# Two transformer blocks on one core: the opening rewritten, and the epsilon of the norms added on VectorE

## The chip, the cores and the metric

The kernel runs on one core of a Trainium2 chip. Its time is the device time of one execution in microseconds, and of several executions the median. Its engines work beside one another and meet at semaphores: TensorE (PE, matrix products and transposes, with weight loads as PEld), VectorE (DVE), ScalarE (ACT), GpSimd (POOL) and SyncE (SP), which here issues DMA transfers.

## The reference, cut to what matters

The input x is 256 tokens by 1024 channels, all in fp32. Two blocks run one after the other; each normalises, mixes and feeds forward with residuals. The first begins like this:

```
def rms_norm(x, gain):
    y = xf * lax.rsqrt(jnp.mean(xf * xf, axis=-1, keepdims=True) + RMS_EPS)
    return y * gain
h = rms_norm(x, g_mix_pre)
q, k, v, p, gu, gv, gates = split(h @ w_in)     # w_in is 1024 x 5376
```

Then come a stick-breaking attention in blocks of 128 tokens, a pooling over several windows, a gated spatial mixing, and a feed-forward part with norms before and behind it (`g_ff_pre`, `g_ff_post`). The second block is a transformer block whose norms are shifted and scaled by rows that come from a condition vector through a 1024-wide matrix (ada).

## The kernel before, in words

The 256 tokens are two tiles of 128 (t = 0, 1), kept token by partition as x0 and x1. A norm goes over one tile: ACT squares two halves of 512 channels with a running sum (`norm_stats`, line 530), POOL adds the two sums and epsilon (line 515) and raises the result to -1/2 (line 518), and DVE multiplies (lines 537 and 542 for a plain norm, 537 and 544 for a shifted one, 551 and 555 for a norm behind a branch). PE then transposes the tile in eight pieces of 128x128 (line 493), since its products want channels on partitions. Each transposed half is split into a high and a low part: hH by ACT (line 487), hL by DVE (line 488).

Weights stream from memory into three slots of 1 MB (`raw`, line 331), in a fixed list. `prep_one` makes of each a high part (ACT, line 352) and a low part (DVE, line 353), in two halves of 128x1024; four slots hold these. A product of fp32 numbers is made of three: high by high, low by high, high by low (lines 441 to 443, and 448 to 450 for the form with tokens on the output's partitions). The ada matrices are no products; DVE accumulates them (line 367).

The framework's scheduler puts the instructions of an engine in order, from the program's own order and costs of its own; slots and semaphores do the rest. Inside `tc.manual_schedule(engines=...)` the engines that are named keep the program's order. All loads go through SP in the order in which they are issued, and a slot's next load is issued when the conversion that reads it is done.

The opening: SP loads x0, then the row `g_mix_pre` spread over 128 partitions (512 KB, line 269), the first quarter of the weights for v, x1 behind it (line 333), and the rest. Then the two tiles are normalised (`make_h`) and the v products run: 48 of 128x512 from two weight slots, whose results are in two banks of PSUM. POOL makes the masks of the pooling part (lines 588 to 596) when the scheduler finds room. Behind v come products for p, gv, u, q, k, then the attention.

Of the kernel before, what the change touches and what calls it, by code (L numbers as in the profile page):

```python
# [105 lines left out]
def net_kernel(ctx: ExitStack, tc: tile.TileContext, I, out):  # L106
# [14 lines left out]
    def T(shape, tag, bufs, dt=F32):  # L121
        if tag in BASE_PAD and tag not in based:
            based.add(tag)
            sb.tile([P, BASE_PAD[tag]], F32, tag="pad" + tag, bufs=1, name=nm("pad"))
        return sb.tile(shape, dt, tag=tag, bufs=bufs, name=nm(tag))
# [7 lines left out]
    def dram(ap, offset, dims):  # L133
        return bass.AP(tensor=ap.tensor, offset=ap.offset + offset, ap=dims)
# [61 lines left out]
    B = {}  # L196
    B["v"] = block512(w_in, 5376, 1024)
    for h in range(2):
        stream[h].parts = [(0, 2), (2, 4)]
        stream[h].loads = [(dram(w_in, (h * 512 + a * P) * 5376 + 1024, [[5376, P], [P * 5376, 2], [1, 512]]), a, a + 2)  # L200
                           for a in (0, 2)]
    ada_want(0, (1, 0, 2, 4, 3, 5))
# [60 lines left out]

    x = [T([P, D], f"x{t}", 1) for t in range(NT)]
    xv = I["x"]
    nc.sync.dma_start(x[0], dram(xv, 0, [[D, P], [1, D]]))

    def bcast_row(tile_ap, vec, off, n, eng=None):
        (eng or nc.sync).dma_start(tile_ap, dram(vec, off, [[0, P], [1, n]]))
# [1 line left out]
    def gain_tile(vec):  # L271
        g = T([P, D], "gb", 2)
        bcast_row(g, vec, 0, D)
        return g

    ident = T([P, P], "ident", 1)
    make_identity(nc, ident)
    g_cur = gain_tile(I["g_mix_pre"])

    neg_half = T([P, 1], "neghalf", 1)  # L280
    nc.vector.memset(neg_half, -0.5)
# [42 lines left out]
    def issue_raw():  # L324
        while st["raw"] < len(stream) and st["raw"] < st["prep"] + RAW_SLOTS:
            it = stream[st["raw"]]
            rt = T([P, 2048], "raw", RAW_SLOTS)
            kc, n = it.shape if isinstance(it, Half) else (4, 512)
            v = rt.rearrange("p (c n) -> p c n", c=kc)
            for ap, a, b in it.loads:  # L330
                nc.sync.dma_start(v[:, a:b, :], ap)
                if st["raw"] == 0 and a == 0:
                    nc.sync.dma_start(x[1], dram(xv, P * D, [[D, P], [1, D]]))
            raws[st["raw"]] = v
            st["raw"] += 1

# [1 line left out]
    ada_tiles = {}  # L338
    ada_ready = []

    def prep_one():
        i = st["prep"]
        it = stream[i]
        v = raws.pop(i)
        if isinstance(it, Half):
            kc, n = it.shape
            h = T([P, kc, n], "wH", W_SLOTS, F32R)
            l = T([P, kc, n], "wL", W_SLOTS, F32R)
            for a, b in it.parts:
                m = (a + b) // 2  # L350
                for p, q in ((a, m), (m, b)) if b - a == kc else ((a, b),):
                    act(h[:, p:q, :], v[:, p:q, :], AF.Copy)  # L352
                    nc.vector.tensor_sub(l[:, p:q, :], v[:, p:q, :], h[:, p:q, :].bitcast(F32))  # L353
            it.H, it.L = h, l
            st["live"].append(it)
        else:
            if it.half == 0:
                ini = ada_init
                nc.sync.dma_start(ini[0:1, :], dram(I["ada_b_2"], it.layer * 6 * D + it.seg * D + it.n * 512,
                                                      [[512, 1], [1, 512]]))  # L360
                acc_cur[0] = T([P, 512], "acc", 1)
                src = ini
            else:
                src = acc_cur[0]
            for c in range(4):
                k = it.half * 4 + c
                stt(acc_cur[0], v[:, c, :], cond[:, k:k + 1], src, op0=ALU.mult, op1=ALU.add)  # L367
                src = acc_cur[0]
            if it.half == 1:
                ah = T([P, 512], "accH", 1, F32R)  # L370
                al = T([P, 512], "accL", 1, F32R)
                act(ah, acc_cur[0], AF.Copy)
                nc.vector.tensor_sub(al, acc_cur[0], ah.bitcast(F32))
                ada_ready.append((it, ah, al, st["gen"]))
        st["prep"] += 1
# [50 lines left out]
    def need(*blocks):  # L426
        pump()
        if any(h.H is None for b in blocks for h in b.halves):
            ada_finish()
            pump()  # L430
        for b in blocks:
            for h in b.halves:
                assert h.H is not None
# [78 lines left out]
    def rstd_of(parts):  # L512
        rs = T([P, 1], "rst", 4)
        if len(parts) == 2:
            nc.gpsimd.tensor_scalar(rs, parts[0], parts[1], EPS, op0=ALU.add, op1=ALU.add)  # L515
        else:
            nc.gpsimd.tensor_scalar(rs, parts[0], EPS, None, op0=ALU.add)
        nc.gpsimd.tensor_tensor(rs, rs, neg_half, op=ALU.pow)
        return rs

# [43 lines left out]

    hk = KM()
    issue_raw()
    for t in range(NT):
        make_h(hk, t, g_cur)
    pump()
    load_cols()  # L570
    load_cond()

    need(B["v"])
    vtok = T([P, NT, 512], "q4", 4)
    va = [bankA(), bankA()]
    for kq in range(4):
        for t in range(NT):
            ts(va[t], hk.h(t), hk.l(t), B["v"], K8[2 * kq:2 * kq + 2], 0, 512, start=(kq == 0), stop=(kq == 3))
    done(B["v"])
    for t in range(NT):  # L580
        act(vtok[:, t, :], va[t], AF.Copy)
# [27 lines left out]
    for g in range(4):  # L609
# [10 lines left out]
    nc.gpsimd.affine_select(tri, tri, pattern=[[-1, P]], base=0, channel_multiplier=1,  # L620
                            compare_op=ALU.is_ge, fill=0.0)


    wsT = T([P, 4, P], "ada5", 1)
    pt = bankB()
# [690 lines left out]
```

## Time and profile before

| | us |
|---|---|
| three runs | 1003.84, 1004.29 (median), 1008.91 |
| profiled execution | 1004.09 |
| its span, from first to last instruction | 1002.4 |
| PE busy in it | 966.3 |
| first transpose on PE | 11.00 |
| first v product | 16.12 |
| first p product | 28.20 |

The span is that of the trace; the execution is 1.69 us longer, with what starts and ends it. The mean granted clock of PE is 0.998 of full speed. The first p product marks the end of the opening: all v products have been issued by then. PE's busy time is not the whole of its span: the difference is idle time before and between instructions, which the waits list by what ended it. Times of places are given from the start of the span.

### The profile page before, as it was taken

The page shows a single profiled execution, that of the slowest core. Times are in us where ns is not written, and L with a number is a line of the kernel's source. Part 1 is how long each engine was busy: PE and PEld are TensorE (multiplying, and loading weights), DVE is VectorE, ACT ScalarE, POOL GpSimd, SP SyncE. Part 2 cuts the span into 40 slices and gives each one's busy share as a digit, 9 for nine tenths or more (in the row PEclk, how much of TensorE's full clock was granted, in tenths as well). Part 3 has the DMA queues.
Part 4 walks back from the last instruction along what each step waited for, and adds up shares of the span by engine and source line. Part 5 has one row for each costly group of instructions (what it writes and reads, how often), then busy time and mean ns, then how long its engine had stood idle before and what let it go on. Part 6 is the DMA issues. An engine that isn't in the chain of part 4 may idle for free.

```text
span 1002.4 us, 14398 instructions
## 1 busy us (share of the span) xinstructions
PE 966.3 (96%) x5733; PEld 837.2 (84%) x5733; DVE 716.6 (71%) x932; ACT 530.4 (53%) x777; POOL 66.6 (7%) x104
## 2 busy tenths in 40 slices
PE   4999999989999999999999999999999999999998
PEld 4999999868899997775778999997876778999996
DVE  6769887788577776889788567768678486665443
ACT  5656664357455455533556455545477456545451
POOL 5102010010000000100000000000330000000000
PEclk9999999999999999999999999999999999999999
DMA  8787686568777885677269777876534246577531
GB/s 270 249 295 251 221 295 207 183 222 307 249 243 283 284 300 204 210 262 274 84 211 305 274 260 252 284 252 210 169 125 169 84 145 233 210 242 252 198 128 43
DMA packets 102192, 223.99 MB, mean 223 GB/s; under 512 B 4332, under 2 KB 8326, under 8 KB 102125
## 3 DMA queue, kind: packets, MB, share of 16 engines
q1 hardware_dynamic: 102124, 223.07, 64.4%
q8 instruction: 45, 0.74, 0.3%
q14 instruction: 23, 0.18, 0.0%
HBM read 221.96 MB, written 1.10 MB: 223 GB/s over the span
## 4 chain that ended last, share of the span: by engine, by line
PE 82%; DVE 8%; POOL 3%; ACT 3%; issue 2%; DMA 1%; POOLq 0%; ACTq 0%; SPq 0%; DVEq 0%
PE A L443 14%; PE A L441 14%; PE A L442 14%; PE B L450 7%; PE B L449 7%; PE B L448 7%; PE A L448 4%; PE A L449 4%; PE A L450 3%; DVE wL L353 3%; ACT wH L352 1%; POOL rst L515 1%; ACT junk L530 1%; PE A L1028 1%; PE B L493 1%
## 5 line engine op out<-in xcount | busy, mean ns | idle before, releaser
L353 DVE TENSOR_TENSOR wL<-raw,wH 128x1024 fp32r<-128x1024 f32 x306 | 362.0, 1221 | 123.4 <-ACT wH L352 122.8
L352 ACT ACTIVATE wH<-raw 128x1024 fp32r<-128x1024 f32 x306 | 308.0, 1049 | 193.8 <-PE A L443 112.2
L450 PE MATMUL B<-hH,wL 128*128 128x256 f32 x576 | 163.0, 283 | 0.0
L449 PE MATMUL B<-hL,wH 128*128 128x256 f32 x576 | 163.0, 283 | 0.0
L448 PE MATMUL B<-hH,wH 128*128 128x256 f32 x576 | 162.9, 283 | 0.0
L441 PE MATMUL A<-wH,hidH 128*128 128x512 f32 x384 | 151.0, 393 | 0.0
L442 PE MATMUL A<-wL,hidH 128*128 128x512 f32 x384 | 150.2, 391 | 0.0
L443 PE MATMUL A<-wH,hidL 128*128 128x512 f32 x384 | 150.1, 391 | 0.0
L367 DVE SCALAR_TENSOR_TENSOR acc<-raw,cond,acc 128x512 f32<-128x512 f32 x168 | 125.9, 750 | 16.4 <-DMA raw<-in_ada_w_dram 13.0
L441 PE MATMUL A<-wH,hH 128*128 128x512 f32 (+1 forms) x336 | 130.5, 388 | 0.5 <-ACT hH L487 0.5
L443 PE MATMUL A<-wH,hL 128*128 128x512 f32 (+1 forms) x336 | 128.8, 383 | 0.2 <-DVE hL L488 0.2
L442 PE MATMUL A<-wL,hH 128*128 128x512 f32 (+1 forms) x336 | 128.8, 383 | 0.0
L449 PEld LDWEIGHTS B<-hL,wH 128*128 128x128 f32 x576 | 110.5, 192 | 0.7
L448 PEld LDWEIGHTS B<-hH,wH 128*128 128x128 f32 x576 | 110.5, 192 | 0.7
L450 PEld LDWEIGHTS B<-hH,wL 128*128 128x128 f32 x576 | 110.5, 192 | 0.0
L441 PEld LDWEIGHTS A<-wH,hidH 128*128 128x128 f32 x384 | 72.5, 189 | 15.4 <-issue 0.8
L443 PEld LDWEIGHTS A<-wH,hidL 128*128 128x128 f32 x384 | 72.5, 189 | 15.3
L442 PEld LDWEIGHTS A<-wL,hidH 128*128 128x128 f32 x384 | 72.6, 189 | 14.6
L448 PE MATMUL A<-hH,wH 128*128 128x256 f32 x272 | 77.8, 286 | 0.0
L449 PE MATMUL A<-hL,wH 128*128 128x256 f32 x272 | 77.0, 283 | 0.0
L450 PE MATMUL A<-hH,wL 128*128 128x256 f32 x272 | 76.9, 283 | 0.0
L441 PEld LDWEIGHTS A<-wH,hH 128*128 128x128 f32 x336 | 63.6, 189 | 13.7 <-issue 1.3
(234 smaller groups left out, 1287.9 us busy)
## 6 DMA issues: line engine op xcount, KB each, us to landing
raw<-in_mlp_w_dram SPq DMA_DIRECT2D x64, 1024.0 KB
raw<-in_ada_w_dram SPq DMA_DIRECT2D x48, 1024.0 KB
raw<-in_w_in_dram SPq DMA_DIRECT2D x19, 1024.0 KB
raw<-in_w_ff_in_dram SPq DMA_DIRECT2D x16, 1024.0 KB
raw<-in_w_ff_out_dram SPq DMA_DIRECT2D x16, 1024.0 KB
raw<-in_attn_w_qkv_dram SPq DMA_DIRECT2D x12, 1024.0 KB
raw<-in_conv_w_in_dram SPq DMA_DIRECT2D x8, 1024.0 KB
ada<-mod SPq DMA_DIRECT2D x24, 256.0 KB
```

What stands on the lines that cost most here:

```text
L352: act(h[:, p:q, :], v[:, p:q, :], AF.Copy)
L353: nc.vector.tensor_sub(l[:, p:q, :], v[:, p:q, :], h[:, p:q, :].bitcast(F32))
L367: stt(acc_cur[0], v[:, c, :], cond[:, k:k + 1], src, op0=ALU.mult, op1=ALU.add)
L441: mm(dst, lh(xc), wh, start=s0, stop=False)
L442: mm(dst, lh(xc), wl, start=False, stop=False)
L443: mm(dst, ll(xc), wh, start=False, stop=s1)
L448: mm(dst, wh, rh(xc), start=(i == 0), stop=False)
L449: mm(dst, wh, rl(xc), start=False, stop=False)
L450: mm(dst, wl, rh(xc), start=False, stop=(i == len(kcs) - 1))
L493: nc.tensor.transpose(pt[:, i * P:(i + 1) * P], src[:, i * P:(i + 1) * P], ident)
L515: nc.gpsimd.tensor_scalar(rs, parts[0], parts[1], EPS, op0=ALU.add, op1=ALU.add)
L530: act(junk(512), p, AF.Square, scale=1.0 / 32.0, accum_out=ss[:, n:n + 1])
```

## The change

It has two parts. The opening is rewritten. The gain row comes as one row of 4 KB, ahead of x0 and x1, which are loaded ahead of all weights. Two matmuls with a row of ones spread it over the 128 partitions into two banks of PSUM (`gp2`), and one DVE instruction per half multiplies x by the reciprocal root and by the gain. PE, DVE and ACT run in the order that is written there, POOL too up to the end of its masks. The first weights are converted in parts, and v products of tile 0 stand between. The other part is in `rstd_of`: the addition of epsilon is on DVE for all its callers, the power stays on POOL.

```diff
--- before.py
+++ after.py
@@ -196,7 +196,6 @@
     B = {}
     B["v"] = block512(w_in, 5376, 1024)
     for h in range(2):
-        stream[h].parts = [(0, 2), (2, 4)]
         stream[h].loads = [(dram(w_in, (h * 512 + a * P) * 5376 + 1024, [[5376, P], [P * 5376, 2], [1, 512]]), a, a + 2)
                            for a in (0, 2)]
     ada_want(0, (1, 0, 2, 4, 3, 5))
@@ -263,7 +262,10 @@
 
     x = [T([P, D], f"x{t}", 1) for t in range(NT)]
     xv = I["x"]
-    nc.sync.dma_start(x[0], dram(xv, 0, [[D, P], [1, D]]))
+    grow = T([1, D], "ada0", 1)
+    nc.sync.dma_start(grow, dram(I["g_mix_pre"], 0, [[D, 1], [1, D]]))
+    for t in range(NT):
+        nc.sync.dma_start(x[t], dram(xv, t * P * D, [[D, P], [1, D]]))
 
     def bcast_row(tile_ap, vec, off, n, eng=None):
         (eng or nc.sync).dma_start(tile_ap, dram(vec, off, [[0, P], [1, n]]))
@@ -275,7 +277,6 @@
 
     ident = T([P, P], "ident", 1)
     make_identity(nc, ident)
-    g_cur = gain_tile(I["g_mix_pre"])
 
     neg_half = T([P, 1], "neghalf", 1)
     nc.vector.memset(neg_half, -0.5)
@@ -329,8 +330,6 @@
             v = rt.rearrange("p (c n) -> p c n", c=kc)
             for ap, a, b in it.loads:
                 nc.sync.dma_start(v[:, a:b, :], ap)
-                if st["raw"] == 0 and a == 0:
-                    nc.sync.dma_start(x[1], dram(xv, P * D, [[D, P], [1, D]]))
             raws[st["raw"]] = v
             st["raw"] += 1
 
@@ -338,7 +337,7 @@
     ada_tiles = {}
     ada_ready = []
 
-    def prep_one():
+    def prep_one(by_part=False):
         i = st["prep"]
         it = stream[i]
         v = raws.pop(i)
@@ -346,13 +345,19 @@
             kc, n = it.shape
             h = T([P, kc, n], "wH", W_SLOTS, F32R)
             l = T([P, kc, n], "wL", W_SLOTS, F32R)
-            for a, b in it.parts:
-                m = (a + b) // 2
-                for p, q in ((a, m), (m, b)) if b - a == kc else ((a, b),):
-                    act(h[:, p:q, :], v[:, p:q, :], AF.Copy)
-                    nc.vector.tensor_sub(l[:, p:q, :], v[:, p:q, :], h[:, p:q, :].bitcast(F32))
             it.H, it.L = h, l
             st["live"].append(it)
+
+            def part(p, q):
+                act(h[:, p:q, :], v[:, p:q, :], AF.Copy)
+                nc.vector.tensor_sub(l[:, p:q, :], v[:, p:q, :], h[:, p:q, :].bitcast(F32))
+
+            m = kc // 2
+            if by_part:
+                st["prep"] += 1
+                return [lambda: part(0, m), lambda: part(m, kc)]
+            for p, q in ((0, m), (m, kc)):
+                part(p, q)
         else:
             if it.half == 0:
                 ini = ada_init
@@ -512,9 +517,9 @@
     def rstd_of(parts):
         rs = T([P, 1], "rst", 4)
         if len(parts) == 2:
-            nc.gpsimd.tensor_scalar(rs, parts[0], parts[1], EPS, op0=ALU.add, op1=ALU.add)
+            vts(rs, parts[0], parts[1], EPS, op0=ALU.add, op1=ALU.add)
         else:
-            nc.gpsimd.tensor_scalar(rs, parts[0], EPS, None, op0=ALU.add)
+            vts(rs, parts[0], EPS, None, op0=ALU.add)
         nc.gpsimd.tensor_tensor(rs, rs, neg_half, op=ALU.pow)
         return rs
 
@@ -564,18 +569,50 @@
 
     hk = KM()
     issue_raw()
-    for t in range(NT):
-        make_h(hk, t, g_cur)
+    vtok = T([P, NT, 512], "q4", 4)
+    va = [bankA(), bankA()]
+    pool_order = tc.manual_schedule(engines={nc.gpsimd.engine})
+    pool_order.__enter__()
+    with tc.manual_schedule(engines={nc.tensor.engine, nc.vector.engine, nc.scalar.engine}):
+        gp2 = [bankB(), bankB()]
+        for n in range(2):
+            mm(gp2[n], ones_r[0:1, :].bitcast(F32), grow[:, half(n)], start=True, stop=True)
+
+        def x_scaled(t, rs):
+            hs = []
+            for n in range(2):
+                h = T([P, 512], "rs", 4)
+                stt(h, x[t][:, half(n)], rs, gp2[n], op0=ALU.mult, op1=ALU.mult)
+                hs.append(h)
+            return hs
+
+        def v_part(t, kq):
+            ts(va[t], hk.h(t), hk.l(t), B["v"], K8[2 * kq:2 * kq + 2], 0, 512, start=(kq == 0), stop=(kq == 3))
+
+        rst = [norm_stats([x[0][:, half(n)] for n in range(2)])]
+        h0 = x_scaled(0, rst[0])
+        rst.append(norm_stats([x[1][:, half(n)] for n in range(2)]))
+        hk.from_token_half(0, 0, h0[0])
+        parts = prep_one(by_part=True)
+        parts[0]()
+        hk.from_token_half(0, 1, h0[1])
+        v_part(0, 0)
+        h1 = x_scaled(1, rst[1])
+        parts[1]()
+        issue_raw()
+        hk.from_token_half(1, 0, h1[0])
+        hk.from_token_half(1, 1, h1[1])
+        v_part(0, 1)
+        v_part(1, 0)
+        v_part(1, 1)
+        parts = prep_one(by_part=True)
+        for i in range(2):
+            parts[i]()
+            for t in range(NT):
+                v_part(t, 2 + i)
     pump()
     load_cols()
     load_cond()
-
-    need(B["v"])
-    vtok = T([P, NT, 512], "q4", 4)
-    va = [bankA(), bankA()]
-    for kq in range(4):
-        for t in range(NT):
-            ts(va[t], hk.h(t), hk.l(t), B["v"], K8[2 * kq:2 * kq + 2], 0, 512, start=(kq == 0), stop=(kq == 3))
     done(B["v"])
     for t in range(NT):
         act(vtok[:, t, :], va[t], AF.Copy)
@@ -620,6 +657,8 @@
     nc.gpsimd.affine_select(tri, tri, pattern=[[-1, P]], base=0, channel_multiplier=1,
                             compare_op=ALU.is_ge, fill=0.0)
 
+
+    pool_order.__exit__(None, None, None)
 
     wsT = T([P, 4, P], "ada5", 1)
     pt = bankB()
```

In the order of DVE in the opening, x_1_63 and x_2_64 are x0 and x1, gb_71 is the spread gain row, wL_149 and wL_132 the low part of the first weights. Before:

```order
L537 TENSOR_TENSOR rs_92<-x_1_63,gb_71 128x512
L537 TENSOR_TENSOR rs_94<-x_1_63,gb_71 128x512
L353 TENSOR_TENSOR wL_149<-raw_83,wH_148 128x1024
L542 TENSOR_SCALAR rs_92<-rs_92,rst_101 128x512
L542 TENSOR_SCALAR rs_94<-rs_94,rst_101 128x512
L537 TENSOR_TENSOR rs_120<-x_2_64,gb_71 128x512
L537 TENSOR_TENSOR rs_122<-x_2_64,gb_71 128x512
L542 TENSOR_SCALAR rs_120<-rs_120,rst_129 128x512
L542 TENSOR_SCALAR rs_122<-rs_122,rst_129 128x512
L488 TENSOR_TENSOR hL_82<-B_106,hH_81 128x4x128
L353 TENSOR_TENSOR wL_149<-raw_83,wH_148 128x1024
```

After, where B_100 and B_101 are the gain in PSUM and rst the norm's statistic:

```order
L520 TENSOR_SCALAR rst_109<-ss_104 128x1
L585 SCALAR_TENSOR_TENSOR rs_112<-x_1_63,rst_109,B_100 128x512
L585 SCALAR_TENSOR_TENSOR rs_114<-x_1_63,rst_109,B_101 128x512
L520 TENSOR_SCALAR rst_121<-ss_116 128x1
L493 TENSOR_TENSOR hL_83<-B_124,hH_82 128x4x128
L353 TENSOR_TENSOR wL_132<-raw_84,wH_131 128x1024
L493 TENSOR_TENSOR hL_83<-B_135,hH_82 128x4x128
L585 SCALAR_TENSOR_TENSOR rs_148<-x_2_64,rst_121,B_100 128x512
L585 SCALAR_TENSOR_TENSOR rs_150<-x_2_64,rst_121,B_101 128x512
L353 TENSOR_TENSOR wL_132<-raw_84,wH_131 128x1024
L493 TENSOR_TENSOR hL_83<-B_156,hH_82 128x4x128
```

The gain product and the scaling are one instruction, the additions of epsilon are DVE's, and the first half's weight subtraction stands behind hL of the first half of tile 0.

In the order of PE at the norm at 511 us of the trace before, A_4785 and A_4812 (after: A_4791 and A_4818) are banks of the second block's products, rs_4733 (after: rs_4739) the tile that waits to be transposed. Before:

```order
L443 MATMUL A_4785<-wH_4683,hL_4640 128x512
L441 MATMUL A_4785<-wH_4683,hH_4639 128x512
L442 MATMUL A_4785<-wL_4684,hH_4639 128x512
L493 MATMUL B_4747<-ident_66,rs_4733 128x128 x4
L443 MATMUL A_4785<-wH_4683,hL_4640 128x512
L493 MATMUL B_4754<-ident_66,rs_4735 128x128 x4
L441 MATMUL A_4812<-wH_4761,hH_4639 128x512
```

After:

```order
L448 MATMUL A_4791<-wH_4689,hL_4646 128x512
L446 MATMUL A_4818<-wH_4767,hH_4645 128x512
L447 MATMUL A_4818<-wL_4768,hH_4645 128x512
L448 MATMUL A_4818<-wH_4767,hL_4646 128x512
L446 MATMUL A_4818<-wH_4767,hH_4645 128x512
L447 MATMUL A_4818<-wL_4768,hH_4645 128x512
L498 MATMUL B_4753<-ident_69,rs_4739 128x128 x4
L448 MATMUL A_4818<-wH_4767,hL_4646 128x512
L498 MATMUL B_4760<-ident_69,rs_4741 128x128 x4
L446 MATMUL A_4818<-wH_4767,hH_4645 128x512
L447 MATMUL A_4818<-wL_4768,hH_4645 128x512
```

Products of the next bank, five of them, and one of the last have moved ahead of the first four transposes.

In the order of ACT at the norm at 204 us of the trace before, junk_2143 and junk_2145 are the squares of x0 (after: 2149 and 2151), hH_2122 (after: hH_2128) is the tile's high part, wH the weights' high parts. Before:

```order
L530 ACTIVATE junk_2143,ss_2142<-x_1_63 128x512
L352 ACTIVATE wH_2166<-raw_1905 128x1024
L530 ACTIVATE junk_2145,ss_2142<-x_1_63 128x512
L352 ACTIVATE wH_2174<-raw_2035 128x1024 x2
L487 ACTIVATE hH_2122<-B_2152 128x4x128
L487 ACTIVATE hH_2122<-B_2159 128x4x128
```

After:

```order
L352 ACTIVATE wH_2172<-raw_1911 128x1024 x2
L535 ACTIVATE junk_2149,ss_2148<-x_1_63 128x512
L535 ACTIVATE junk_2151,ss_2148<-x_1_63 128x512
L352 ACTIVATE wH_2180<-raw_2041 128x1024 x2
L352 ACTIVATE wH_2263<-raw_2178 128x1024 x2
L492 ACTIVATE hH_2128<-B_2158 128x4x128
L492 ACTIVATE hH_2128<-B_2165 128x4x128
```

Two weight copies, wH_2263 from raw_2178, now stand ahead of the two copies of hH.

## Rows read from the trace of the kernel before

**Rows 1.** Page, part 1: busy time by engine, share of the span, instructions.
```profile
PE 966.3 (96%) x5733; PEld 837.2 (84%) x5733; DVE 716.6 (71%) x932; ACT 530.4 (53%) x777; POOL 66.6 (7%) x104
```

**Rows 2.** Waits of PE by line: us in total, times, longest.
```profile
PE B L493 <- DVE rs L542: 16.7, 4, 11.0
PE B L493 <- DVE rs L544: 6.9, 5, 1.6
...
PE B L1050 <- DVE hidL L1044: 1.6, 2, 1.5
...
PE A L441 <- ACT hH L487: 0.5, 1, 0.5
```

**Rows 3.** Timeline of the opening: start, us, instruction [idle before <-releaser].
```profile
1.24 0.42 SPq L269 DMA_DIRECT2D gb<-in_g_mix_pre_dram  x1
...
4.49 0.63 ACT L530 ACTIVATE junk<-x 128x512 bf16<-128x512 f32 x1 [2.42 <-DMA x<-in_x_dram]
...
6.06 0.30 POOL L515 TENSOR_SCALAR rst<-ss 128x1 f32<-128x1 f32 x1 [4.27 <-ACT junk L530]
...
6.60 1.29 DVE L537 TENSOR_TENSOR rs<-x,gb 128x512 f32<-128x512 f32 x2 [5.24 <-DMA gb<-in_g_mix_pre_dram]
6.80 0.93 POOL L518 TENSOR_TENSOR rst<-rst,neghalf 128x1 f32<-128x1 f32 x1
...
9.04 1.48 DVE L353 TENSOR_TENSOR wL<-raw,wH 128x1024 fp32r<-128x1024 f32 x1 [1.15 <-ACT wH L352]
...
11.00 1.97 PE L493 MATMUL B<-ident,rs 128*128 128x128 f32 x8 [11.00 <-DVE rs L542]
...
12.15 0.60 ACT L487 ACTIVATE hH<-B 128x512 fp32r<-128x512 f32 x1 [0.40 <-PE B L493]
...
14.50 1.97 PE L493 MATMUL B<-ident,rs 128*128 128x128 f32 x8 [1.53 <-DVE rs L542]
...
16.12 0.78 PE L441 MATMUL A<-wH,hH 128*128 128x512 f32 x1
...
18.40 0.40 PE L443 MATMUL A<-wH,hL 128*128 128x512 f32 x1
...
22.86 0.15 DVE L601 TENSOR_SCALAR ci<-pos 128x2 f32<-128x2 f32 x1
...
28.20 0.28 PE L441 MATMUL A<-wH,hH 128*128 128x256 f32 x1
```

**Rows 4.** Timeline of PE at four later norms.
```profile
204.08 1.09 PE L493 MATMUL B<-ident,rs 128*128 128x128 f32 x8 [2.38 <-DVE rs L542]
...
398.19 1.29 PE L493 MATMUL B<-ident,rs 128*128 128x128 f32 x8 [1.52 <-DVE rs L544]
...
414.21 0.63 PE L493 MATMUL B<-ident,rs 128*128 128x128 f32 x4 [1.51 <-DVE rs L544]
...
511.53 0.66 PE L493 MATMUL B<-ident,rs 128*128 128x128 f32 x4 [1.53 <-DVE rs L544]
```

**Rows 5.** Timelines of POOL and DVE: two held POOL instructions, one consumer.
```profile
411.22 1.41 POOL L515 TENSOR_SCALAR rst<-ss 128x1 f32<-128x1 f32 x1 [2.46 <-ACT junk L530]
...
411.33 1.22 DVE L353 TENSOR_TENSOR wL<-raw,wH 128x1024 fp32r<-128x1024 f32 x1
...
510.72 1.42 DVE L544 SCALAR_TENSOR_TENSOR rs<-rs,rst,ada 128x512 f32<-128x512 f32 x2 [0.85 <-POOL rst L518]
...
720.46 1.21 DVE L353 TENSOR_TENSOR wL<-raw,wH 128x1024 fp32r<-128x1024 f32 x1
...
720.63 1.14 POOL L1149 TENSOR_SCALAR ssq<-ssq 128x8 f32<-128x8 f32 x1 [5.95 <-DVE ssq L1148]
```

**Rows 6.** Timelines of DVE and ACT around the norm at 204.
```profile
195.28 0.75 DVE L367 SCALAR_TENSOR_TENSOR acc<-raw,cond,ini 128x512 f32<-128x512 f32 x1 [4.88 <-DMA raw<-in_ada_w_dram]
...
204.34 3.49 DVE L353 TENSOR_TENSOR wL<-raw,wH 128x1024 fp32r<-128x1024 f32 x3
...
209.11 1.09 ACT L487 ACTIVATE hH<-B 128x512 fp32r<-128x512 f32 x2 [5.15 <-PE A L442]
```

## Prediction, made before the changed kernel ran

> **What bounds the kernel now.** The first view is the busy time by engine: TensorE (PE) works 966.3 of 1002.4 us, VectorE (DVE) 716.6, ScalarE (ACT) 530.4 [rows 1]. The change removes no product, so it can only shorten what PE idles, or lengthen it. The second view is the list of what PE waited for. The transposes of line 493, which begin every normalised token tile, waited 16.7 us in four places for the plain norm (line 542) and 6.9 us in five for the shifted one (line 544); line 1050 waited 1.6 us [rows 2]. These 25.2 us are about all that is within reach. The third view, the timeline of the opening, shows 12.53 of the 16.7: PE idle until 11.00, and 1.53 us more before 14.50 [rows 3]. The fourth, PE's rows at the later norms, has 2.38 us at 204.08, 1.52 at 398.19, 1.51 at 414.21 and 1.53 at 511.53 [rows 4]. By subtraction from rows 2 there remain 1.8 us at token tile 1 behind 204.08 (16.7 - 12.53 - 2.38) and 2.3 us at two more norms like that of 511.53, at 699 and 822 (6.9 - 1.52 - 1.51 - 1.53).
>
> The profiled run took 1004.09 us, 1.69 more than its span; the median of the runs is 1004.29, so the sum, made against 1004.09, holds for either.
>
> **The opening.** Before, the first transpose hangs on one chain: the squares of x0 from 4.49, POOL's addition at 6.06, its power at 6.80, drawn out to 0.93 us beside DVE's product with the broadcast gain (6.60, itself 5.24 us behind the gain's load), and then a weight subtraction (9.04, 1.48 us) that DVE does ahead of the scaling [rows 3]. After token tile 1 has gone the same way, v products start at 16.12, and the 48 are done at 28.20, where the p products begin [rows 3].
>
> After, with the same durations: the gain row's issue ahead of x0 costs 0.42 (1.24 [rows 3]), so the squares start near 4.9 and end near 6.4. The addition on DVE takes 0.15 (the narrow row at 22.86), the power 0.56 to 0.93: 7.2 to 7.5. The gain's two matmuls are over by then, since they need 4 KB and a constant. Fused scalings take 0.71 each (two in 1.42 at 510.72 [rows 5]); the first is done at 8.0 to 8.3. hH begins 1.15 after its transposes do (11.00 to 12.15 [rows 3]), 9.15 to 9.5; the first half of the weights is copied 0.5 later, in 1.05, and subtracted in 1.22 to 1.48 (411.33 [rows 5], 9.04). PE has its second v product at S = 12.0 to 12.6.
>
> From S on nothing stops PE: h1's halves come at S+1.4 and S+2.1, the second half of the first weights at S+3.4, hL of tile 1 at S+4.2 and S+5.1, and ahead of the first product that needs these last stand 5 products, 8 transposes and 6 products, some 5.3 us. Products take 0.456 apiece first (16.12 to 18.40, five), which is 1.2 GHz, and 0.2275 afterwards (18.40 to 28.20, 43 of them), which is 2.4 GHz. So from S: 5 x 0.456 + 1.62 for the transposes (14.50 to 16.12) + 42 x 0.2275 = 13.5, ending at 25.5 to 26.1. The clock is the open part. Before, it rose at 18.40, behind a wait that ended at 14.50. If it rises at 18.40 again, the products from S+3.9 to there run at half rate, which adds 1.0: 26.5 to 27.1. I take 26.1, between the two: a gain of **2.1 us**, bounds 1.1 and 2.7.
>
> What hides the rest: POOL's masks, which move behind both powers, have their readers near 30 us; the loads behind (cond, columns, gm gain) move forward one by one with SP's queue, since each raw load is released by a conversion and each conversion by products. None of the waits of rows 2 that I name lies between 28.20 and 204, so nothing there runs against a fixed time and the lead should carry.
>
> **The addition on DVE.** At the norms behind the opening, line 515's addition leaves POOL. There it takes 0.30 with nothing beside it (6.06 [rows 3]) but 1.41 at 411.22, where a DVE subtraction runs from 411.33 for 1.22: it ends 0.1 after the subtraction [rows 5]. A POOL instruction beside a two-input DVE instruction is held. On DVE the addition takes 0.15 and nothing holds it. At 398 no subtraction stands between it and its consumer; that saves about 0.2, and the new order has one more product ahead of the transposes (0.23): **0.5** gained (bounds 0.3 and 0.8).
>
> Elsewhere the new order has a subtraction between the addition and its consumer, so the power meets it instead. The pattern stands in a row of the attention part: line 1149, on POOL, starts 0.17 after a subtraction (720.46, 1.21) and lasts 1.14 [rows 5]. Before, the consumer started 0.85 after DVE's last instruction (510.72 [rows 5]). After, it starts behind 0.07 for the addition, 1.14 of subtraction, and the power's tail, 0.44 plus a hand-over (6.80 + 0.93 against 7.29, where the first of the two multiplications from 6.60 ends [rows 3]): 1.69, so 0.84 later. Against that, more products stand ahead of the transposes, at 0.2275 each: at 511 six more (1.37), so 0.5 gained; at 699 the same; at 822 one more, and DVE takes the halves in another order, which I also put at 0.5; at 414 eight more (1.82), which leaves 0.98 of gain, of which I take 0.65, since only four transposes go at 414.21 (x4 [rows 4]) and the other four wait again. Line 1050 gains 0.14. Together **2.3 us** (0.65 + 0.14 + 3 x 0.5). The lower bound of each is nothing, the upper its whole idle time: 1.5, 0.15, and 3.8 for the three.
>
> At 204 and 219 it is different. PE's order has fifteen products instead of six ahead of tile 0's transposes (2.05 us of cover) and ten instead of six ahead of tile 1's (0.9); with 0.84 of delay, idle times of 2.38 and 1.8 become 1.2 and 1.7. But ACT has two weight copies ahead of the two hH. Their load is issued when a slot is free, after the first of the three subtractions from 204.34, near 205.5; 1 MB at the mean 223 GB/s is 4.7 us [rows 1, 6], so it lands near 210.2, and two copies end near 212.2. Before, hH started at 209.11, after 5.15 us of waiting for PE [rows 6], and PE then waited 0.5 us for it [rows 2]. So it is some 3.1 late, less the products moved: 2.6 us of wait. Altogether 1.2 + 1.7 + 2.6 = 5.5 against 2.38 + 1.8 + 0.5 = 4.7: **0.8 us lost** (bounds: 1.9 lost if the load takes a microsecond more, 0.7 gained if it takes 1.5 less).
>
> A rule of the Trainium skill bears on the held power: "SBUF — State Buffer", section "Who interferes with whom", says that a VectorE instruction with two SBUF inputs and a GpSimd instruction that reads SBUF contend, and that in such contention the one that issues first has the shared port for its whole instruction while the other fully blocks. The rows at 411.22 and 720.63 agree that the later one waits to the other's end [rows 5]. By the rule the power would also run its full 0.56 after the subtraction, where the row at 6.80 shows 0.44: 0.12 more at each of five places, and 1000.6 in the end.
>
> Sum: 2.1 + 0.5 + 2.3 - 0.8 = 4.1; 1004.09 - 4.1 = **1000.0**.
>
> **Rivals.**
> *The power is not held.* If it gets in ahead of the subtraction, the products cover all idle time at 414, 477, 511, 699 and 822 (1.5 + 0.15 + 3.8, of which 1.1 stays at 511 and 822, where 1.4 and one product's 0.2 are all the cover), 0.5 is saved at 398, and 204 comes out even: 4.85 + 2.1 = 6.95, so **997.1**. For: the power's operands are ready 0.15 after the addition starts, and the subtraction follows on DVE only then. Against: at 6.80 the held one was under way next to a multiplication already, and 720.63 was held too.
> *The opening's lead is eaten.* PE starts earlier, but a load or a constant sets the time before 88 us, where DMA has as much to bring as before; 1004.09 - 2.0 = **1002.1**. For: all loads together take as long as before, 224 MB at 223 GB/s [rows 1]. Against: rows 2 list no wait of PE for a load.
> *ACT's order at 204 stops PE.* Both hH stand behind two copies of a weight whose load is not there. The row at 195.28 shows DVE 4.88 us behind such a load [rows 6]. If this one is as late, the loss there is 0.8 + 4.9 = 5.7, and the held powers leave nothing at the other norms: 1004.09 - 2.1 + 5.7 = **1007.7**. It ends on the slow side from a load that lands 4.1 us later than I take it. Against: the slot is free 3.5 us before hH can start anyway.
>
> **Chances.** Forecast .50, first rival .21, second .19, third .10. A measurement of this kernel can tell 0.5%, 5.0 us, from no change. Faster by that is below 999.1: .15 of the forecast (its own spread is 998.4 to 1001.6) and .18 of the first rival, .33. Slower is above 1009.1: half of the third, .05. Same .62. The range reaches from just beyond the first rival, 996.3, to the second's upper end, 1003.8 (the opening at nothing and the norms at 0.3).
>
> **What would show it.** First v product near 11.0, second near 12.3, p products from 26.1, and the same 2 us of lead at 88 and 200. Powers of 1.2 to 1.6 where a subtraction follows the addition, 0.56 at 398. PE idle about 1.0 at 398, 0.9 at 414, 1.0 at 511, 1.3 at 699 and 822 together, and near 209 a wait of 2 to 3 us for hH. The forecast is wrong if powers take 0.56 everywhere (first rival), if the lead shrinks before 88 (second), or if PE stops over 4 us near 209 (third).

## The result, and the profile after

The changed kernel takes 999.79 us (median of ten runs, 997.38 to 1002.13) against 1005.18 for the kernel before in its ten runs: a ratio of 0.9943, with a 95% interval of 0.9927 to 0.9960. It is faster, by 4.0 to 7.3 us. The profiled execution took 999.48 us with a span of 997.8; that of before had 1002.4. The prediction of 1000.0 is met; the sum behind it is met less well, since two of its terms were off by 2.1 and 2.6 us in opposite directions.

The list of PE's waits after is the answer to [rows 2].

```profile
PE B L498 <- DVE rs L549: 3.8, 5, 1.2
...
PE B L498 <- DVE rs L547: 2.6, 2, 1.8
...
PE B L1089 <- DVE hidL L1083: 1.7, 3, 1.4
PE B L715 <- DVE rs L685: 1.6, 1, 1.6
```

The shifted norm fell from 6.9 to 3.8 us (line 544, now 549), the plain one behind the opening from 4.2 (2.38 and 1.8) to 2.6 (line 547). Line 715 is new: PE waits 1.6 us for a gated product that it never waited for before.

The opening on the timeline, against [rows 3]:

```profile
6.24 0.21 DVE L520 TENSOR_SCALAR rst<-ss 128x1 f32<-128x1 f32 x1 [4.88 <-ACT junk L535]
6.54 0.55 POOL L523 TENSOR_TENSOR rst<-rst,neghalf 128x1 f32<-128x1 f32 x1 [4.25 <-DVE rst L520]
...
7.13 1.41 DVE L585 SCALAR_TENSOR_TENSOR rs<-x,rst,B 128x512 f32<-128x512 f32 x2 [0.67 <-POOL rst L523]
...
7.93 1.97 PE L498 MATMUL B<-ident,rs 128*128 128x128 f32 x8 [1.75 <-DVE rs L585]
...
9.08 0.60 ACT L492 ACTIVATE hH<-B 128x512 fp32r<-128x512 f32 x1 [1.36 <-PE B L498]
...
10.68 0.80 PE L446 MATMUL A<-wH,hH 128*128 128x512 f32 x1 [0.78 <-ACT wH L352]
...
12.00 0.79 PE L447 MATMUL A<-wL,hH 128*128 128x512 f32 x1 [0.53 <-DVE wL L353]
...
14.30 1.91 PE L498 MATMUL B<-ident,rs 128*128 128x128 f32 x8
...
16.27 0.40 PE L447 MATMUL A<-wL,hH 128*128 128x512 f32 x1
...
25.60 0.28 PE L446 MATMUL A<-wH,hH 128*128 128x256 f32 x1
```

First v product at 10.68 (11.0 was said), second at 12.00 (12.0 to 12.6), p products from 25.60 (26.1), which is 2.60 us earlier than before. The step from 0.43 to 0.23 us per product came at 16.27, not at 18.40, one product behind the transposes of tile 1 that begin at 14.30.

The other norms on PE, against [rows 4]:

```profile
204.21 1.09 PE L498 MATMUL B<-ident,rs 128*128 128x128 f32 x8 [1.83 <-DVE rs L547]
...
207.83 0.50 PE L446 MATMUL A<-wH,hH 128*128 128x512 f32 x1 [0.45 <-ACT hH L492]
...
217.05 1.09 PE L498 MATMUL B<-ident,rs 128*128 128x128 f32 x8 [0.73 <-DVE rs L547]
...
395.80 1.29 PE L498 MATMUL B<-ident,rs 128*128 128x128 f32 x8 [1.19 <-DVE rs L549]
...
412.44 0.63 PE L498 MATMUL B<-ident,rs 128*128 128x128 f32 x4 [0.55 <-DVE rs L549]
...
508.61 0.66 PE L498 MATMUL B<-ident,rs 128*128 128x128 f32 x4 [0.91 <-DVE rs L549]
...
695.13 1.07 PE L498 MATMUL B<-ident,rs 128*128 128x128 f32 x6 [0.25 <-DVE rs L549]
...
817.84 0.66 PE L498 MATMUL B<-ident,rs 128*128 128x128 f32 x4 [0.85 <-DVE rs L549]
```

At 398 the idle time fell from 1.52 to 1.19, at 414 from 1.51 to 0.55, at 511 from 1.53 to 0.91, and at 699 and 822 it is 1.10 together, after 2.3. At 204 and 219 the idle time is 1.83 + 0.45 + 0.73 = 3.0, after 4.8.

Idle times do not say where time is kept, so I took the start of the same PE instruction in both traces, before less after, as the lead of a kernel at that place. For the changed kernel it reads: 2.60 us at the first p product, 1.39 at the line-700 products (55.67 before), 3.25 at 224.23, 2.35 behind 248, 2.61 at 405, 3.58 at 419, 4.29 at 518, 4.6 from 828 to the end. So 1.2 us of the opening were lost near 47, 1.6 to 1.9 were won at 204 to 220, 0.9 lost near 245, 3.0 won at the norms from 398 on and 0.3 at an ada product (532.27 before, whose idle time fell from 0.51 to 0.18), and 1.0 lost near 733 to PE's clock. The clock also fell near 264 in both kernels, which cancels (the last section).

### The profile page after: what moved, and what is told of

Read it like the earlier page. It is cut to its first block, busy times and chain, and to the rows that moved or that the text cites. A ratio compares the mean times of both kernels' runs of the same rounds, so it can differ in the third digit from the quotient of the medians.

```text
span 997.8 us, 14401 instructions
## 1 busy us (share of the span) xinstructions
PE 972.2 (97%) x5737; PEld 839.4 (84%) x5737; DVE 717.8 (72%) x948; ACT 529.1 (53%) x776; POOL 59.6 (6%) x84
## 4 chain that ended last, share of the span: by engine, by line
PE 76%; DVE 12%; ACT 3%; issue 3%; DMA 3%; POOL 2%; POOLq 0%; SPq 0%; ACTq 0%; DVEq 0%
PE A L448 13%; PE A L447 13%; PE A L446 13%; PE B L455 7%; PE B L454 7%; PE B L453 7%; DVE wL L353 5%; PE A L453 3%; PE A L454 3%; PE A L455 3%; ACT wH L352 2%; POOL rst L523 1%; DMA raw<-in_ada_w_dram 1%; DVE acc L372 1%; PE A L1067 1%
## 5 line engine op out<-in xcount | busy, mean ns | idle before, releaser
L352 ACT ACTIVATE wH<-raw 128x1024 fp32r<-128x1024 f32 x306 | 308.1, 1050 | 196.4 <-PE A L448 107.5
```

## The experiments

Ten kernels, each run beside the kernel before. The ratio is to before, with its 95% interval; the last three columns are leads in us, each from the one profiled execution, at 55.67, 242.43 and 919.34 us of before.

| | median us | ratio | at 56 | at 242 | end |
|---|---|---|---|---|---|
| changed kernel | 999.79 | 0.9943 (0.9927 to 0.9960) | 1.4 | 3.3 | 4.6 |
| e1 norms only | 1004.39 | 0.9996 (0.9981 to 1.0011) | -3.7 | -1.5 | 1.6 |
| e2 opening only | 1001.25 | 0.9966 (0.9954 to 0.9978) | 2.3 | 2.4 | 3.4 |
| e3 sum added on ACT | 1000.41 | 0.9967 (0.9947 to 0.9987) | 2.6 | 5.0 | 4.4 |
| e4 gating gain early | 999.27 | 0.9942 (0.9920 to 0.9963) | 3.2 | 5.4 | 2.7 |
| e5 = e4, third ada half later | 997.42 | 0.9924 (0.9908 to 0.9940) | 3.0 | 4.9 | 7.6 |
| e6 = e4, first ada half later | 997.26 | 0.9920 (0.9905 to 0.9935) | 3.3 | 5.3 | 6.1 |
| e7 weights ahead of hH | 998.89 | 0.9935 (0.9921 to 0.9949) | 3.6 | 5.8 | 4.3 |
| e8 before, third ada half later | 1004.56 | 0.9992 (0.9979 to 1.0004) | 0.5 | 0.6 | 1.0 |
| e9 changed, third ada half later | 997.45 | 0.9923 (0.9907 to 0.9938) | 2.0 | 4.1 | 7.1 |
| e10 all three edits | 994.60 | 0.9890 (0.9874 to 0.9905) | 5.0 | 7.2 | 9.5 |

### The two parts by themselves: e1 and e2

e1 is the kernel before with

```diff
-            nc.gpsimd.tensor_scalar(rs, parts[0], parts[1], EPS, op0=ALU.add, op1=ALU.add)
+            vts(rs, parts[0], parts[1], EPS, op0=ALU.add, op1=ALU.add)
```

and the same for one part; e2 is the changed kernel with the opposite edit. Behind 100 us e1 has the changed kernel's order on DVE, PE and ACT, e2 that of before.

> The kernel before with one edit: the addition of epsilon on DVE (all callers), the old opening. On DVE, PE and ACT its order behind 100 us is that of the changed kernel. Theory (the two parts are independent): from the leads read between the two traces, 1.6 us at 204 to 220, about 2.5 us over the norms at 398, 414, 477, 511, 699 and 822: 4.1 us faster than before, ratio 0.996. The load of the weights that both hH copies stand behind is issued near 199 us and lands near 205, ahead of hH; the powers that meet a subtraction last 1.4 to 1.5 us. Rival (the gain at 204 needs the opening's earlier loads): hH waits for ACT's copies as forecast, 0.8 us lost there, and 1.7 us faster in all, ratio 0.998.

> The changed kernel with the addition of epsilon back on POOL: the opening alone; its order behind 100 us is that of before. Theory (the lead of the opening is cut at 47 us, where PE's product with the gated tile waits for DVE): p products near 25.8 us, a PE stop of 1.2 to 1.6 us near 47, a lead of 1.4 us from 55 us to the end, ratio 0.9986; near 204 the four idle times of before, 4.8 us together. Rival (the lead carries): 2.6 us to the end, ratio 0.9974. Both: this and the norms alone add up to the whole change, 0.9943.

e1 missed its ratio, and not at the norms. Behind the opening it gains 5.3 us on before (from -3.7 to 1.6; PE's clock fell in before near 264 and in e1 near 736, which cancels), and at 204 it shows the changed kernel's picture: 1.48, 0.45 and 0.74 us of idle time, hH not held by ACT's copies. So the gain at 204 does not need the new opening, and the rival is out. But the old opening loses 3.7 us by the same edit, 2.9 of them by the first p product:

```profile
12.93 0.20 DVE L515 TENSOR_SCALAR rst<-ss 128x1 f32<-128x1 f32 x1
...
17.38 0.62 DVE L542 TENSOR_SCALAR rs<-rs,rst 128x512 f32<-128x512 f32 x1 [2.51 <-POOL rst L518]
...
16.80 0.55 POOL L518 TENSOR_TENSOR rst<-rst,neghalf 128x1 f32<-128x1 f32 x1
...
18.05 1.12 PE L493 MATMUL B<-ident,rs 128*128 128x128 f32 x4 [1.91 <-DVE rs L542]
```

These are DVE, POOL and PE of e1 from 12.9 to 18 us. The addition is done at 13.13, but POOL takes the power up at 16.80, since its own order has masks ahead of it, from 8.68 on without a break; DVE then waits 2.51 us for the power, and tile 1 is transposed at 18.05, 3.6 us later than before. In the changed kernel POOL has both powers ahead of the masks (6.54 above, tile 1's at 8.74). So the addition on DVE costs the old opening much of what it wins at the norms, and the new opening's order on POOL takes that cost away. Whether the two parts add up is not settled: by the leads at the end they do nearly, 1.6 + 3.4 = 5.0 against 4.6; by the ratios it is 0.4 + 3.4 us against 5.7, each uncertain by 1.2 to 1.7.

e2 has no stop near 47 and a lead of 2.3 to 2.4 us from 56 to 242: the lead of the opening alone does carry that far, and its expected stop was wrong. Its ratio of 0.9966 goes with the rival's 0.9974, which the interval holds, and not with 0.9986. The stop at 47 thus belongs to the two parts together (e1 stops 0.81 us at the same product, but there DVE waits 2.40 us for the gating gain's own load):

```profile
42.87 0.20 DVE L522 TENSOR_SCALAR rst<-ss 128x1 f32<-128x1 f32 x2
44.10 2.36 DVE L353 TENSOR_TENSOR wL<-raw,wH 128x1024 fp32r<-128x1024 f32 x2 [1.03 <-ACT wH L352]
46.38 0.87 DVE L685 SCALAR_TENSOR_TENSOR rs<-rs,rst,ada 128x256 f32<-128x256 f32 x2
...
43.01 2.00 ACT L352 ACTIVATE wH<-raw 128x1024 fp32r<-128x1024 f32 x2 [1.58 <-DMA raw<-in_w_in_dram]
...
46.91 1.27 PE L715 MATMUL B<-ada,rs 128*64 128x128 f32 x14 [1.59 <-DVE rs L685]
```

DVE and ACT of the changed kernel: two weight subtractions (44.10) stand ahead of the gated product of line 685, and they wait for ACT's copy, which waited 1.58 us for its load (43.01). In e2 the same two subtractions start at 43.10, and PE does not wait.

### Is the held power what leaves the idle time: e3

```diff
-            vts(rs, parts[0], parts[1], EPS, op0=ALU.add, op1=ALU.add)
+            se = T([P, 1], "se", 4)
+            vts(se, parts[0], EPS, None, op0=ALU.add)
+            act(rs, parts[1], AF.Identity, bias=se)
```

> The changed kernel; epsilon is added on DVE to the first half's sum alone, while ACT squares the second half, and ACT adds the two sums (128x1, with the first as its bias); the power stays on POOL. So no DVE instruction stands between the last square and the power, and the power meets whatever DVE has in hand, not the next subtraction. Theory (the held power is what leaves idle time at 204, 414, 511, 699 and 822): DVE's consumer starts 0.5 to 0.6 us after the instruction that held the power; PE idle at 204 and 217 falls from 2.6 to about 1.3 us, at 414, 511 and 822 from 2.3 to under 1; 1.5 to 2.5 us faster than the changed kernel, ratio to before 0.992. Rival (the idle time is set by which products the order puts ahead of the transposes): no difference from the changed kernel, 0.994, or 0.5 us slower by ACT's additions in its queue.

The power is held, as forecast. These are POOL and DVE of the changed kernel at 202, answering to [rows 5], and its plain power at 390:

```profile
201.88 0.20 DVE L520 TENSOR_SCALAR rst<-ss 128x1 f32<-128x1 f32 x1
202.00 1.21 DVE L353 TENSOR_TENSOR wL<-raw,wH 128x1024 fp32r<-128x1024 f32 x1
203.66 0.49 DVE L547 TENSOR_SCALAR rs<-rs,rst 128x512 f32<-128x512 f32 x1 [0.45 <-POOL rst L523]
...
202.16 1.47 POOL L523 TENSOR_TENSOR rst<-rst,neghalf 128x1 f32<-128x1 f32 x1 [3.99 <-DVE rst L520]
...
390.84 0.55 POOL L523 TENSOR_TENSOR rst<-rst,neghalf 128x1 f32<-128x1 f32 x1 [174.37 <-DVE rst L520]
```

It lasts 1.47 us beside the subtraction and ends 0.42 behind it; DVE idles 0.45 us for it, and the consumer starts 1.78 behind the addition (1.69 was said). Eight of the twenty powers last 1.39 to 1.47, those with nothing beside them 0.55. In e3 the held ones are shorter in the main (0.66 to 1.41), and the idle time at 204 and 217 falls to 1.03 and 0.67, at 511 from 0.91 to 0.50, at 822 from 0.85 to 0.54. But at 414 it is 0.75 plus 0.40 for a weight, at 699 0.91 after 0.25: the order that the scheduler makes of it takes back elsewhere what the power gives. At 242 its lead is 5.0 us, 1.7 above the changed kernel, and its ratio is not better. So the power is held as I said, but the time that e3 was to give did not come (0.9967 where 0.992 was expected). That the order takes it back is read off these rows, and was not tried.

### What cuts the lead: e4 to e9

e4 takes the stop at 47 away: the gating gain's load is issued in the opening, and the gated product comes ahead of one of the two subtractions.

```diff
     pump()
+    gmc = T([P, 1024], "ada3", 1)
+    bcast_row(gmc[:, 256:512], I["gm_gain"], 0, 256)
     load_cols()
...
-    bcast_row(gmg, I["gm_gain"], 0, 256)
```

> The changed kernel; the load of the gating gain (128 KB) is issued right behind the opening's loads instead of near 40 us, and DVE has the gated product (line 685) ahead of one of the two weight subtractions that it stood behind. Theory (the stop at 47 us is that product behind two subtractions, whose copies waited 1.6 us for a load): PE's stop near 47 falls from 1.6 to 0.4 us, and 1.1 us more of the opening's lead is there at 88 us and at the end: ratio to before 0.993. Rival (loads set the time there): PE stops elsewhere before 88 us, the lead there stays at 1.4, ratio 0.9943 as for the changed kernel.

The stop went, the lead at 56 is 3.2 us and at 242 5.4, and the median is near the changed kernel's. In the profiled execution, at 1001.38 us the slowest of e4's six (three took 997.5 to 997.7), the lead was lost at one place:

```profile
241.86 1.54 DVE L372 SCALAR_TENSOR_TENSOR acc<-raw,cond,acc 128x512 f32<-128x512 f32 x2 [0.61 <-DMA raw<-in_ada_w_dram]
...
246.16 0.80 PE L386 MATMUL B<-accH,onesr 128*128 128x512 f32 x1 [3.06 <-ACT accH L377]
...
245.49 0.51 PE L386 MATMUL B<-accH,onesr 128*128 128x512 f32 x1 [0.26 <-ACT accH L377]
246.22 0.50 PE L387 MATMUL B<-accL,onesr 128*128 128x512 f32 x1 [0.22 <-DVE accL L378]
...
241.19 1.54 DVE L372 SCALAR_TENSOR_TENSOR acc<-raw,cond,acc 128x512 f32<-128x512 f32 x2 [0.77 <-DMA raw<-in_ada_w_dram]
...
233.59 0.37 SPq L332 DMA_DIRECT2D raw<-in_ada_w_dram  x1
```

The first two are e4, the others the changed kernel. PE's product with the ada accumulation stands at 245.5 and 246.2: 0.26 us of waiting with a lead of 3.3, 3.06 with 5.4. ACT's copy behind the wait needs the accumulation, whose load was issued at 233.59 and let DVE start at 241.19. From 234 to 245 DMA is busy 96 to 100% in the changed kernel and in before, at about 350 GB/s. So I took it that the load cannot come earlier, and that a lead is cut there. Other kernels do not bear that out:

```profile
248.34 0.39 PE L381 MATMUL B<-accH,onesr 128*128 128x512 f32 x1
...
250.29 0.50 PE L381 MATMUL B<-accH,onesr 128*128 128x512 f32 x1 [0.31 <-ACT accH L372]
...
245.93 0.39 PE L386 MATMUL B<-accH,onesr 128*128 128x512 f32 x1
...
243.85 0.45 PE L386 MATMUL B<-accH,onesr 128*128 128x512 f32 x1
...
220.63 0.37 SPq L332 DMA_DIRECT2D raw<-in_ada_w_dram  x1
...
228.72 0.75 DVE L372 SCALAR_TENSOR_TENSOR acc<-raw,cond,ini 128x512 f32<-128x512 f32 x1 [3.04 <-DMA raw<-in_ada_w_dram]
...
230.00:235.00 5.00, 5.00 (x26) 4.14 (x25) 5.00 (x7) 2.42 (x4) 0.00 (x0) 1.00 0.29 71
```

These are the same product in before, e1, e2 and e3, then e4 somewhat earlier (the last two figures of its window are the share of DMA time and GB/s). e1, with the old opening and a lead of -1.5 us, stops there too and loses 1.0 us; e2, with the new opening alone and a lead of 2.4, does not wait, nor does e3 with 5.0. So the stop of the changed kernel comes with the order that the second part makes behind 100 us, which e1 shares, and not with a PE that is early. In e4 the stop is longer because DVE waited 3.04 us for the ada load before this one, 8.1 us after its issue at 220.63 (in the changed kernel DVE used it without a wait 5.1 us after its issue). DMA was then 29% busy from 230 to 235, and the next ada load was issued at 234.48, 0.9 us later than in the changed kernel, though PE was 2.1 us ahead. Why the load before took so long is open. e5, e6, e8 and e9 move one ada half out of this stretch by one number of a table:

```diff
-'ff': (1, 1, 1, 1, 1, 1, 1, 1, 1, 0, 1, ...)
+'ff': (1, 1, 0, 1, 1, 1, 1, 1, 1, 1, 1, ...)
```

(e6: the first number instead of the third). e7 leaves the table alone and enlarges the opening's lead: `parts[0]()`, the first weights' first half, is called ahead of `hk.from_token_half(0, 0, h0[0])`.

> The kernel with the early gating gain (e4); of the ada halves that are streamed between the feed-forward weights, the third is moved to the place that had none (one number of the table PUSH, ff index 2 to 9). So the load of 1 MB that is issued near 234 us, and the ada product that PE had at 245 behind it, stand later. Theory (the lead behind 220 us is cut at 245, where PE's ada product waits for an accumulation whose load comes late, between 234 and 245 where DMA moves 330 to 395 GB/s): no wait of PE for the ada product near 245, the lead of 4.9 to 5.4 us at 224 is still over 4.5 at 290, and the kernel is 1.5 to 2.5 us faster than e4's fast runs (997.5): 995 to 996, ratio to before 0.991. Rival (the stop only moves: another load or ada product takes its place): PE waits as long between 245 and 300, ratio 0.994.

> As e5, but the first of the ada halves moves (ff index 0 to 9), so every ada load up to there comes one place later and the stretch from 190 us has 1 MB less to load. Theory as for e5: the wait at 245 is gone, and the load of the weights behind the norm at 204 comes earlier still; ratio 0.991. Rival: 0.994.

> The changed kernel; in the opening ACT copies the first half of the first weights ahead of the first hH instead of behind it, and DVE subtracts it ahead of the first hL. Theory (the second v product waits for the subtraction, which waits for ACT's copy behind hH): second v product near 11.0 instead of 12.0, p products 0.5 to 1 us earlier, and of that nothing at the end, since 245 cuts it: ratio 0.994 as for the changed kernel. Rival (the lead of the opening carries): 0.9935.

> The kernel before with e5's one number of the table alone (the third ada half of the feed-forward part one place later). Theory (before, PE came to its ada product at 248 after the accumulation was done, so there is nothing to win without a lead): no difference, ratio 1.000 within 0.0015. Rival (the table's number is a gain of its own, by less load between 205 and 250): 2 us faster, ratio 0.998.

> The changed kernel with the same one number. Theory (its lead of 3.2 us at 224 is cut to 2.4 at 248): no wait of PE for an ada product near 245, the lead at 290 is 0.5 to 0.9 us larger, ratio 0.9935. Rival: as the changed kernel, 0.9943, with the wait at another place.

```profile
245.40 0.49 PE L386 MATMUL B<-accH,onesr 128*128 128x512 f32 x1 [2.67 <-ACT accH L377]
...
254.91 0.40 PE L386 MATMUL B<-accH,onesr 128*128 128x512 f32 x1
```

The rows are e7, then e5. e7's lead of 5.8 us at 242 ran into the same stop as e4's (2.67 us of waiting at 245.40, with DVE 3.15 us behind a load at 228.46) and was 2.5 behind it; PE's clock then took 1.5 more. By the lead the first theory holds, and the ratio allows either. In e5 the ada product stands at 254.91 without a wait, 5.0 us of lead are there at 270, and the ratio is 0.9924, less of a gain than the 0.991 expected. In e6, at 0.9920, a wait of 0.19 at 232 is left. The kernel before does not gain by the same number (0.9992, interval over 1): PE does not wait there. The changed kernel does: 0.9923 against 0.9943, though the intervals overlap, and at 242 to 260 no wait is left in its trace. That PE's stop near 245 is a wait for this ada half, and goes when the half stands later, is shown; that the full DMA stretch cuts a lead is not. How much of the gain of e9 over the changed kernel is the 0.9 us of lead, and how much is that e9's profile happens to have no slow stretch of PE, is not shown either.

### The three edits together: e10

> The changed kernel with the three edits together: early gating gain (e4), third ada half later (e5), weights ahead of hH in the opening (e7). Theory (the leads add up once nothing cuts them at 245): 0.7 us more lead at 55 us than e5's 3.0, kept to the end: 996.5 us, ratio 0.9915. Rival (loads of the first 60 us set the time once the opening is faster, as the wait of 0.88 us for the spatial weights at 40 us in e7): as e5, 0.9924.

994.60 us, ratio 0.9890 (0.9874 to 0.9905): below both values that I gave, and the fastest kernel here, 5.2 us under the changed one. The lead at 56 us is 5.0, of which e5 had 3.0; the second v product starts at 10.45, and products run at 0.23 us from 11.22 on, ahead of tile 1's transposes instead of behind them. PE does not wait near 245.

## Why the prediction was right or wrong

**The opening, 2.1 us to the first p product: right, 2.6 measured.** Its chain came out within 0.3 us step by step (transposes from 7.93, where the scaled half was put at 8.0 to 8.3; hH at 9.08; second product at 12.00). What was left over is the clock: it rose 2.1 us earlier than in before, and I had halved that chance. That is one execution's luck: with the same order of v products, e9's p products start at 25.52 and e5's, whose clock rose later, at 26.25.

**That the lead carries: right for the opening alone, wrong for the two parts together.** "None of the waits of rows 2 that I name lies between 28.20 and 204, so nothing there runs against a fixed time and the lead should carry." In e2 it does, from 56 through 245. In the changed kernel it failed twice. Near 47 us 1.2 of the 2.6 went, because DVE's order put the gated product behind two subtractions that wait for a load; PE had no wait there before, but only because it came later. Near 245 0.9 us went to a load, and that with the second part's order: e1 loses 1.0 there with a lead of -1.5. I had put that part at nothing between the norms. The second rival (a load sets the time before 88 us) holds for the 1.2 us near 47 and has no place for the 0.9. That no wait of PE for a load is listed said nothing: PE waits for ACT, which waits for DVE, which waits for the load.

**The addition on DVE at 398 and the five later norms, 0.5 + 2.3 us: right.** The idle time fell by 0.33, 0.96, 0.62 and 1.2 (699 and 822 together), 3.1 us, of which the leads show 3.0. Line 1050 kept its long wait (1.40 after 1.47, where 0.14 of gain was said). Powers of 1.2 to 1.6 where a subtraction follows: 1.39 to 1.47, eight times. The first rival, that the power is not held, is out by the same rows.

**204 and 219, 0.8 us lost: wrong, 1.6 to 1.9 won.** The failed step is "their load is issued when a slot is free, after the first of the three subtractions from 204.34, near 205.5".

```profile
197.02 0.75 DVE L372 SCALAR_TENSOR_TENSOR acc<-raw,cond,acc 128x512 f32<-128x512 f32 x1
...
197.79 0.37 SPq L332 DMA_DIRECT2D raw<-in_w_ff_in_dram  x1
...
203.03 2.01 ACT L352 ACTIVATE wH<-raw 128x1024 fp32r<-128x1024 f32 x2 [0.60 <-DMA raw<-in_w_ff_in_dram]
207.18 1.09 ACT L492 ACTIVATE hH<-B 128x512 fp32r<-128x512 f32 x2 [2.14 <-PE A L447]
```

DVE, SP and ACT of the changed kernel. The fourth accumulation of an ada matrix, which stood at 207.74 before, stands at 197.02, ahead of the consumer that waits for the power, and the load is issued 0.02 us after it ends, 7.8 us earlier than before. It lands by 203.03, both copies are done at 205, and hH waits for PE, 2.14 us, as in [rows 6], not for ACT. I had read the order of ACT and taken the loads' times from before, where I should have followed what the same new order did to the instruction that frees the slot. The load's length was near: 4.7 us said, from a mean of 223 GB/s that stands on the page of before and not in [rows 1], and 5.2 at most here (197.79 to 203.03). The third rival fell with it.

**The sum.** 2.6 - 1.2 + 1.8 - 0.9 + 3.0 = 5.3 in the leads; 4.6 in the profiled pair, with the 0.3 at 532 and the 1.0 that the clock took near 733; 0.9943 of 1005.18, 5.7 us, by the ratio. The forecast of 4.1 (2.1 - 0.8 + 2.8) had errors of +0.5, -2.1, +2.6 and +0.2 in it, in this order, and the two large ones nearly cancel: that the time came so near 1000.0 is in part luck.

**The held power's tail.** The Trainium skill ("SBUF — State Buffer", "Who interferes with whom") has the later of the two wait for the whole of the other instruction. The rows agree that it waits for the end, but with 0.42 us left to run after it (202.16 + 1.47 against 202.00 + 1.21), not its full 0.55; the measured tail is close to the 0.44 of 6.80 in [rows 3]. The row at 411.22, which I read with the rule, is no clean case: POOL's instruction starts 0.11 us ahead of the subtraction at 411.33, while a product of DVE with two inputs still runs (to 411.42).

## What to carry to other kernels

A lead won early has to be followed through every place where something behind PE waits for a load, also where PE waits for nothing today: the wait can appear because PE comes earlier (near 47 us), or because another engine's new order moves the load (near 245). Run each part alone before you lay a stop to the lead: here e1 has the stop near 245 without any lead, and e2 has the lead without the stop. When one instruction moves to another engine, what it frees or delays there (a slot's last reader, the head of an in-order queue such as POOL's masks) moves loads and waits that the edit does not name; read the load's issue from the new order of its slot's last reader. An edit that is near nothing alone (0.9996 for the addition) may still gain beside another that takes an obstacle out of its way (0.9966 without it, 0.9943 with it, in intervals that overlap).

## What the runs showed of the hardware

PE's granted clock fell to half for short stretches while PE was fully busy, and not at the same places in every kernel.

```profile
264.00:268.00 4.00, 4.00 (x11) 3.12 (x11) 3.93 (x6) 2.39 (x5) 0.00 (x0) 0.57 0.91 320
...
256.00:266.00 10.00, 10.00 (x38) 6.80 (x37) 8.06 (x9) 7.37 (x11) 0.00 (x0) 0.83 0.67 224
...
730.00:737.00 7.00, 5.16 (x24) 4.06 (x25) 6.06 (x21) 6.70 (x22) 0.00 (x0) 0.76 0.00 0
...
256.00:266.00 10.00, 10.00 (x36) 6.39 (x35) 8.24 (x10) 5.77 (x10) 0.00 (x0) 1.00 0.71 251
```

These are one window of before, two of the changed kernel and one of e9 (the third figure from the end is the clock). Before ran at 0.57 of full speed from 264 to 268 without a wait just ahead of it. The changed kernel ran at 0.83 over 256 to 266, also without, and at 0.76 over 730 to 737, behind a wait of 1.8 us (before has the same wait at 736.91 and kept its clock). e9 kept its clock in both places. By the leads such a stretch costs 1.0 us (the changed kernel near 733) to 1.6 (before near 264). In e4 the clock was 0.67 over 244 to 248 and 0.65 over 248 to 254, around the wait of 3.06 us, and took another 2.8 us; in e6 it was 0.66 over 256 to 266 without a wait. What sets it off is open: it was not tried.

The runs of one kernel spread over 4 to 5 us (997.4 to 1002.1 for the changed one), nearly as much as the whole change moves. The clock is not all of that: with the same mean granted clock of 0.998, runs of the changed kernel took 997.70, 999.85 and 1000.77. So a lead tells where the time went in one execution, and medians of several runs tell what a step is worth.
